# Two small layout changes and another issuer for ten small transfers in a two-block transformer kernel

## The chip, the cores and the metric

The kernel is written in Bass with its Tile layer for one Trainium2 chip, and runs on 1 core. The metric is device time in microseconds (us) of one execution; the kernel before takes 1630.53 us, the median of 3 runs. TensorE (PE) does the matrix products, VectorE (DVE) and ScalarE (ACT) the element-wise work, GpSimd (POOL) little. SyncE (SP), ScalarE and GpSimd also issue DMA transfers; "SPq", "ACTq" and "POOLq" in the rows are these issues.

## The reference

256 tokens of width 1024 pass two blocks, in float32. The first block:

```python
sh1, sc1, g1, sh2, sc2, g2 = adaln(c, w_mod, b_mod)
x = x + g1 * (concat(diff_attention, window_attention) @ w_out)
h = modulate(rmsnorm(x, norm2_g), sh2, sc2)
x = x + g2 * moe(h)          # 32 experts, the best 4 for each token
x = rmsnorm(x, final_g)
# moe, for an expert e and its tokens:
h = xb @ w_gu[e] + b_gu[e]                      # 1024 -> 2048
g = minimum(h[:, ::2], 7.0); lin = clip(h[:, 1::2], -7.0, 7.0)
y = (g * sigmoid(1.702 * g) * (lin + 1.0)) @ w_dn[e] + b_dn[e]
```

The second block is attention of three kinds (blocked, windowed, and over 256 rows of a memory `mem`), three gates, and a feed-forward part of width 2816 with a depthwise convolution:

```python
kv_me = rmsnorm(mem, norm_mem) @ w_mem_kv
s = q @ k.T * scale + bias_table[bucket(distance)]      # rel_bias
u = causal_depthwise_conv(h @ w_ffn_up, ffn_conv_w, ffn_conv_b)
y = (gelu(u_gate) * u_val) @ w_ffn_down
```

What matters here: each of the 32 experts has 8 MB of gate and up weights and 4 MB of down weights, which are all read once, 384 MB. What the second block needs of `mem`, `ffn_conv_w`, `ffn_conv_b` and `rel_bias` is small.

## The kernel before

The experts run in 16 pairs (`pair(i, bgs)`, L1419, called from the loop at L1566). A pair's two experts stand side by side in the two column halves of TensorE, with 64 slots of tokens each. For 8 values of k, 8 products (4 column groups for 2 experts, L1438) are summed in `gu`; then the activation (`swiglu_chunk`, L1163), the turning of the result, 4 steps of the down products (`dn`, L1456), and in the next pair the `combine` of the rows into the tokens (L1249).

The weights come through one ring (`Ring`, L60 to L115). A tile is 128 partitions x 8192 bytes, 1 MB; a pair needs 16 of gate and up and 8 of down, and four more tiles carry `w_mem_kv`. SyncE issues each tile's load at L99 as soon as a slot of one of the ring's pools is free (`pump`), in the order in which the products use them. The pools in the experts' part are `ra` (3 slots), `rx` (1), `rk` (1), `rb` (8, on the other side of the on-chip memory) and `rc` (3).

A transfer that SyncE or ScalarE issues signals its end on one of eight semaphores. Both engines' transfers take these in turn, in the order of the program, and a transfer waits until the one before it on the same semaphore has landed. GpSimd's transfers have eight others.

Beside the products a list of generators (`bgs`) does one step in each k step of a pair. Three of them matter here. `mem_prep` (L1263) begins in pair 1: it loads `mem` in two pieces of 128 x 1024 (`mrow`, L1268), scales its rows on VectorE (L1272 to L1276) and turns them on TensorE. `mem_kv` uses four of the ring's tiles in pairs 1 to 7. `consts_late` (L1310) is put in at pair 9 and comes to run in pairs 12 and 13: it loads the convolution's weights and bias in two halves of 88 x 128 (`V`, L1316) into a buffer that the marks `S` also use, and TensorE turns each (L494); then it loads `rel_bias` (`rb`, 32 x 16), a table `hot` (32 x 384) and `off` (16 x 384), multiplies (L1328), adds (L1329) and stores the result to `scr_bias` (L1330). All ten of these transfers are issued by ScalarE. `overflow` (L1333), after pair 0, stands under a condition that isn't met with these inputs.

Where the ring's slots lie follows from what is allotted before them: the small constants (`const`) on the one side, and `g2b` (a row of gates for all partitions, L1021) on the side of `rb`.

Of the kernel before, what the change touches and what calls it, by code (L numbers as in the profile page):

```python
# [10 lines left out]
F32 = mybir.dt.float32  # L11
F32R = mybir.dt.float32r
BF16 = mybir.dt.bfloat16
# [6 lines left out]
P = 128  # L20
D = 1024
KD = D // P
T = 256
E = 32
# [155 lines left out]
def body(tc, I, out):  # L180
# [3 lines left out]
    vec, act, pe, pool = nc.vector, nc.scalar, nc.tensor, nc.gpsimd  # L184

    def sb(stack, name, bufs=1, side=None):
        return stack.enter_context(tc.tile_pool(name=name, bufs=bufs, side=side, reuse_waits="tile"))
# [4 lines left out]
    def bc(ap1d, n, parts=P):  # L192
        return bass.AP(tensor=ap1d.tensor, offset=ap1d.offset, ap=[[0, parts], [1, n]])
# [13 lines left out]
    def rsqrt_col(dst, src, n=1, scale=1.0 / D):  # L207
        nwt[0] ^= 1
        t = newton[:, nwt[0]]
        rsqrt(dst, src, scale, (t[:, 0, :n], t[:, 1, :n]))  # L210
# [16 lines left out]
    const = sb(ex, "const")  # L227
# [220 lines left out]
    for names in ((("n1", I["norm1_g"], 8), ("bm", I["b_mod"], 40)),  # L448
                  (("n2", I["norm2_g"], 8), ("pre", I["norm_mix_pre_2"], 8), ("fpre", I["norm_ffn_pre_2"], 8),
                   ("nmem", I["norm_mem_2"], 8), ("fg", I["final_g"], 8), ("mpost", I["norm_mix_post_2"], 8), ("sub", I["subln_g"], 1))):  # L450
        V = r1.tile([sum(n for _, _, n in names), P], F32, name=f"V{len(vrows) + 1}")
# [13 lines left out]
    vec.tensor_scalar(identb, jp, 0.0, None, op0=ALU.is_equal)  # L465
    before = const.tile([P, P], BF16, name="before")
    vec.tensor_scalar(before, jp, 0.0, None, op0=ALU.is_gt)
    maskw = const.tile([P, 2, P], BF16, name="maskw")
    vec.tensor_scalar(maskw[:, 0, :], jp, 0.0, NEG, op0=ALU.is_gt, op1=ALU.mult)
    vec.tensor_scalar(maskw[:, 1, :], jp, 0.0, NEG, op0=ALU.is_lt, op1=ALU.mult)  # L470
    onesb = const.tile([P, P], BF16, name="onesb")
# [7 lines left out]
    slot = const.tile([P, SLOTS], F32, name="slot")  # L479
# [13 lines left out]
    def tp(dst, src, n=P):  # L493
        pe.transpose(dst, src, ident[:src.shape[0], :src.shape[0]])  # L494

    scrb = nc.dram_tensor("scr_bias", (16, 384), F32, kind="Internal").ap()
# [516 lines left out]
    aux = g2b = ringB_stack = None  # L1013

    def other_weights():

        nonlocal aux, g2b, ringB_stack
        rp.close()
        aux = sb(ex, "aux", side="right")
        spl.open("wo", (aux, 2), most=0)  # L1020
        g2b = aux.tile([P, D], F32, name="g2b", tag="g2b")  # L1021
        pool.dma_start(g2b, bc(I["b_mod"][0, 5120:6144], D))
        ringB_stack = ExitStack()
        ringB = sb(ringB_stack, "ringB", bufs=8, side="right")
        ring.open("rb", ringB, 8, ("qmb", 0))
        ring.pump()
        yield
# [18 lines left out]
    def warms():  # L1046
        while True:
# [3 lines left out]
    threads = {"m": mod1, "c": scale_shift(), "h": h_steps(), "1": ka_steps(0), "2": ka_steps(1), "d": small_loads(), "v": lambdas(),  # L1051
               "P": proj(), "M": mods(), "S": da_scores(), "T": da_turn(), "V": da_values(), "N": da_norm(), "W": wa_scores(),
               "s": da_probs(), "w": wa_probs(), "p": splits(), "f": flushes(), "y": warms(), "R": more_slots(), "B": other_weights(),
               "K": da_parts(), "Q": wa_parts(), "U": wa_turn(), "Z": wa_values(), "O": w_out_steps(), "X": x_turn()}

# [92 lines left out]

    vec.scalar_tensor_tensor(rk, pr[:, 0:2 * E].rearrange("p (i e) -> p i e", i=2), 1.0, sel, op0=ALU.add, op1=ALU.mult)
    vec.tensor_scalar(rk, rk, -1.0, None, op0=ALU.add)  # L1150
    cnt = const.tile([P, 4, E], F32, name="cnt")
    vec.tensor_copy(cnt[:, 0, :], pr[:, 2 * E:3 * E])
    st1.close()

# [3 lines left out]
    def misc(name="ms"):  # L1158
        return ps2.tile([P, 512], F32, name=name, tag="ms", bufs=2)
# [25 lines left out]
    xg, GT, SG, gcol = {}, {}, {}, {}  # L1185
# [30 lines left out]
    def gather(i):  # L1216

        S, G = SG.pop(i)
        xg[i] = x = l2.tile([P, KD, P], F32, name="xg", tag=f"p{i % 2}")
        for q in range(2):  # L1220
            pt = misc() if i or q else gub("ms")
            for k in range(4):
                kk = q * 4 + k
                for t in range(2):
                    pe.matmul(pt[:, k * P:(k + 1) * P], lhsT=u[:, t, kk * P:(kk + 1) * P], rhs=S[:, t, :],  # L1225
                              start=t == 0, stop=t == 1)
            for k in range(4):
                kk = q * 4 + k
                act.activation(x[:, kk, :], pt[:, k * P:(k + 1) * P], AF.Identity, scale=A2c[:, kk:kk + 1], bias=B2c[:, kk:kk + 1])  # L1229
            yield  # L1230
        pt = misc()
        if G is None:

            for t in range(2):
                tp(pt[:, t * P:(t + 1) * P], S[:, t, :])
            for t in range(2):
                pe.matmul(pt[:, T:T + 2], lhsT=S[:, t, :], rhs=ge[:, t, 2 * i:2 * i + 2], start=t == 0, stop=t == 1)
            gt = l2.tile([P, T], F32R, name="GT", tag="GT", bufs=2)
            gcol[i] = gcols[i % 2]
            for ee in range(2):  # L1240
                vec.tensor_copy(gcol[i][64 * ee:64 * ee + 64], pt[64 * ee:64 * ee + 64, T + ee:T + ee + 1])
        else:
            for t in range(2):
                tp(pt[:, t * P:(t + 1) * P], G[:, t, :])
            gt = l2.tile([P, T], F32, name="GT", tag="GT", bufs=2)
        act.activation(gt, pt[:, 0:T], AF.Copy)
        GT[i] = gt
# [14 lines left out]
    def mem_prep():  # L1262
        nonlocal memT  # L1263
        memT = aux.tile([P, KD, T], F32, name="memT", tag="ws", bufs=2)
        ms = const.tile([P, 4], F32, name="msum")
        rows_ = [l2.tile([P, D], F32, name="mrow", tag=t) for t in ("pT0", "p2")]
        for i in range(2):
            act.dma_start(rows_[i], I["mem_2"][0, i * P:(i + 1) * P, :])  # L1268
        yield
        for i, j in enumerate(rows_):  # L1270
            sq = l2.tile([P, D], F32, name="mj", tag="pT2")
            vec.tensor_tensor(sq, j, j, ALU.mult)  # L1272
            vec.tensor_reduce(ms[:, i:i + 1], sq, AX.X, ALU.add)
        rsqrt_col(ms[:, 2:4], ms[:, 0:2], 2)
        for i, j in enumerate(rows_):
            vec.tensor_scalar(j, j, ms[:, 2 + i:3 + i], None, op0=ALU.mult)  # L1276
        yield
        for i, j in enumerate(rows_):
            for q in range(2):
                pt = misc()  # L1280
                for k in range(4):
                    tp(pt[:, k * P:(k + 1) * P], j[:, (q * 4 + k) * P:(q * 4 + k + 1) * P])
                gn = colv[:, rows["nmem"]][:, q * 4:q * 4 + 4, None].to_broadcast([P, 4, P])
                vec.tensor_tensor(memT[:, q * 4:q * 4 + 4, i * P:(i + 1) * P], pt.rearrange("p (k t) -> p k t", k=4), gn, ALU.mult)
                yield
# [23 lines left out]
    def consts_late():  # L1309
        ap = I["ffn_conv_w_2"]  # L1310
        for half in range(2):
            V = l2.tile([88, P], F32, name="V2", tag="S", bufs=2)
            for q in range(2):
                n = half * 2 + q
                src = I["ffn_conv_w_2"][0, n] if n < 3 else I["ffn_conv_b_2"][0]
                act.dma_start(V[q * 44:q * 44 + 44, :], bass.AP(tensor=src.tensor, offset=src.offset, ap=[[P, 44], [1, P]]))  # L1316
            pt = misc()
            tp(pt[:, 0:88], V)
            vec.tensor_copy(conv[:, half * 2:half * 2 + 2, :], pt[:, 0:88].rearrange("p (a c) -> p a c", a=2))
            yield  # L1320
        rb = l2.tile([32, 16], F32, name="rb", tag="g", bufs=2)
        act.dma_start(rb, I["rel_bias_2"])
        hot = l2.tile([32, 384], F32, name="hot", tag="pT0")
        act.dma_start(hot, I["k_hot"])
        off = l2.tile([16, 384], F32, name="off", tag="pT2")
        act.dma_start(off, I["k_off"])
        pt = misc()
        pe.matmul(pt[0:16, 0:384], lhsT=rb, rhs=hot, start=True, stop=True)  # L1328
        vec.tensor_tensor(off, off, pt[0:16, 0:384], ALU.add)  # L1329
        act.dma_start(scrb, off)  # L1330
        yield

    def overflow():  # L1333
        nj = nc.values_load(njob[0:1, 0:1], min_val=0, max_val=15)
        with tc.If(nj > 0):
            jt = const.tile([P, 6], F32, name="jt")
            vec.memset(jt[:, 0:1], 0.0)
            eio = const.tile([P, E], F32, name="eio")
            pool.iota(eio, pattern=[[1, E]], base=0, channel_multiplier=0, allow_small_or_imprecise_dtypes=True)
            pio = const.tile([P, 1], F32, name="pio")  # L1340
            pool.iota(pio, pattern=[[0, 1]], base=0, channel_multiplier=1, allow_small_or_imprecise_dtypes=True)
            with tc.For_i(0, nj, 1):
# [219 lines left out]
    njob = const.tile([P, 1], I32, name="njob")  # L1562
    gate_values()
    SG[0] = S0, None
    gcols = [const.tile([P, 1], F32, name=f"gcol{n}") for n in range(2)]
    gather0 = gather(0)  # L1566
    next(gather0)
    bgs = []
# [413 lines left out]
    for c in range(4):  # L1982
        for m in range(2):
# [7 lines left out]
            f = 2 * c + m  # L1991
# [184 lines left out]
```

## Time and profile before

| what | value |
|---|---|
| median of 3 runs | 1630.53 us (1629.62 to 1631.3) |
| the profiled execution | 1631.8 us, span 1630.0 us |
| granted TensorE clock, mean | 0.984 of full speed |
| TensorE busy | 1565.6 us, 96% of the span |
| VectorE, ScalarE, GpSimd busy | 686.0, 487.1, 34.2 us |
| moved by DMA | 524.95 MB, mean 322 GB/s |

The page divides the span into 40 slices of 40.75 us, with a digit or a rate for each. The timeline's rows give the start, the duration, the engine, the line, the operation, the output and inputs, and behind them in brackets the idle time ahead of the instruction and what released it. A busy TensorE need not be at its peak: products that wait a little for each other, or run at a lower clock, look busy too. The share of all the span hides that the kernel has stretches of different kinds, so the windows below are cut by time.

### The profile page before, as it was taken

How to read it: one execution, taken by the hardware profiler on the slowest of the kernel's cores; microseconds unless marked ns; L12 is line 12 of the kernel's file. 1: busy time of each engine (PE TensorE's matmuls, PEld its weight loads, DVE VectorE, ACT ScalarE, POOL GpSimd, SP SyncE). 2: the span in 40 equal slices, each digit the busy share in tenths (PEclk: the TensorE clock that was granted, in tenths of full speed). 3: DMA queues.
4: the chain of work that ended last, by engine and by line, in shares of the span. 5: the costliest groups of instructions: out<-in, count | busy, mean ns of one | idle time of the engine just before them, and what ended most of it. 6: DMA issues, size and time to landing. Idle time of an engine off the chain costs nothing.

```text
span 1630.0 us, 23439 instructions
## 1 busy us (share of the span) xinstructions
PE 1565.6 (96%) x9625; PEld 948.4 (58%) x9625; DVE 686.0 (42%) x1431; ACT 487.1 (30%) x996; POOL 34.2 (2%) x39
## 2 busy tenths in 40 slices
PE   8999999899999999999999987999999999999997
PEld 6887773334433444434443432333479999899996
DVE  5877732331222212212212211122146686778786
ACT  4565532011111101101101110111045455555553
POOL 1000000000000000000000000000011001100000
PEclk9999999899999999999999997999999999999999
DMA  9758879899999999999999999899986447826651
GB/s 330 220 174 266 304 303 365 345 412 420 420 415 420 420 415 420 421 416 420 420 421 420 420 419 391 356 419 421 420 266 206 124 137 198 236 80 188 196 167 70
DMA packets 187546, 524.95 MB, mean 322 GB/s; under 512 B 11142, under 2 KB 129484, under 8 KB 138540
## 3 DMA queue, kind: packets, MB, share of 16 engines
q1 hardware_dynamic: 183600, 518.31, 83.1%
q10 hardware_dynamic: 3212, 4.14, 0.8%
q8 instruction: 77, 1.26, 0.3%
q0 software_dynamic: 624, 0.97, 0.2%
q14 instruction: 33, 0.27, 0.0%
HBM read 522.31 MB, written 1.07 MB: 321 GB/s over the span
## 4 chain that ended last, share of the span: by engine, by line
PE 68%; DMA 11%; DVE 1%; ACT 1%; issue 0%; POOL 0%; ACTq 0%; DVEq 0%; SPq 0%; POOLq 0%
PE gu L1438 23%; PE dn L1456 10%; DMA ra<-in_w_gate_up_dram 3%; PE pj L223 3%; PE pj L224 3%; PE pj L225 3%; PE ms L1225 3%; PE pv L224 3%; PE pv L223 3%; PE pv L225 3%; DMA rb<-in_w_gate_up_dram 2%; PE ms L1255 2%; PE po L224 2%; PE po L223 2%; PE po L225 2%; PE ms L494 1%
## 5 line engine op out<-in xcount | busy, mean ns | idle before, releaser
L1438 PE MATMUL gu<-rb,xg 128*64 128x512 f32 x1080 | 343.3, 612 | 0.8 <-DMA rb<-in_w_gate_up_dram 0.8
L216 DVE TENSOR_TENSOR ws<-ra,ws 128x1024 fp32r<-128x1024 f32 x146 | 176.5, 1240 | 48.2 <-ACT ws L213 48.2
L1438 PEld LDWEIGHTS gu<-rb,xg 128*64 128x64 f32 x1080 | 101.4, 140 | 146.6 <-issue 135.9
L1438 PE MATMUL gu<-ra,xg 128*64 128x512 f32 x384 | 169.1, 600 | 3.3 <-DMA ra<-in_w_gate_up_dram 2.7
L213 ACT ACTIVATE ws<-ra 128x1024 fp32r<-128x1024 f32 x146 | 148.9, 1055 | 64.9 <-PE pj L225 31.8
L1438 PE MATMUL gu<-rc,xg 128*64 128x512 f32 x424 | 164.7, 602 | 0.4 <-DMA rc<-in_w_gate_up_dram 0.4
L1229 ACT ACTIVATE xg<-ms,mcol 128x128 f32<-128x128 f32 x128 | 48.3, 458 | 381.5 <-PE ms L1225 381.5
L1456 PE MATMUL dn<-rb,aT 128*64 128x512 f32 x552 | 159.8, 597 | 0.0
L1257 DVE TENSOR_TENSOR X<-X,ms 128x512 f32<-128x512 f32 x60 | 41.2, 688 | 249.0 <-PE ms L1255 248.9
L1463 DVE SCALAR_TENSOR_TENSOR o<-dn,gcol,g2b 128x512 f32<-128x512 f32 x30 | 22.5, 751 | 212.2 <-PE dn L1456 212.2
L223 PE MATMUL pv<-fh,ws 128*128 128x256 f32 x352 | 100.2, 285 | 0.7 <-ACT fh L2023 0.7
L224 PE MATMUL pv<-fl,ws 128*128 128x256 f32 x352 | 99.6, 283 | 0.1
L225 PE MATMUL pv<-fh,ws 128*128 128x256 f32 x352 | 99.6, 283 | 0.0
L1456 PEld LDWEIGHTS dn<-rb,aT 128*64 128x64 f32 x552 | 49.3, 137 | 68.8 <-issue 66.8
L1456 PE MATMUL dn<-rc,aT 128*64 128x512 f32 x224 | 86.4, 596 | 0.0
L1438 PEld LDWEIGHTS gu<-ra,xg 128*64 128x64 f32 x384 | 46.5, 137 | 66.2 <-issue 57.9
L223 PE MATMUL pj<-hTh,ws 128*128 128x256 f32 x296 | 84.9, 287 | 0.0
L224 PE MATMUL pj<-hTl,ws 128*128 128x256 f32 x296 | 83.0, 280 | 0.0
L225 PE MATMUL pj<-hTh,ws 128*128 128x256 f32 x296 | 82.8, 280 | 0.0
L1438 PEld LDWEIGHTS gu<-rc,xg 128*64 128x64 f32 x424 | 47.4, 137 | 56.4 <-issue 51.2
L1225 PEld LDWEIGHTS ms<-S,u 128*128 128x128 f32 x512 | 59.6, 191 | 25.1 <-issue 25.1
L1438 PE MATMUL gu<-rx,xg 128*64 128x512 f32 x152 | 71.1, 597 | 0.0
(526 smaller groups left out, 2871.5 us busy)
## 6 DMA issues: line engine op xcount, KB each, us to landing
rb<-in_w_gate_up_dram SPq DMA_DIRECT2D x135, 1024.0 KB, 19.8
rb<-in_w_down_dram SPq DMA_DIRECT2D x68, 1024.0 KB, 19.8
rc<-in_w_gate_up_dram SPq DMA_DIRECT2D x53, 1024.0 KB, 19.9
ra<-in_w_gate_up_dram SPq DMA_DIRECT2D x48, 1024.0 KB, 15.1
rc<-in_w_down_dram SPq DMA_DIRECT2D x27, 1024.0 KB, 19.8
ra<-in_w_in_dram SPq DMA_DIRECT2D x26, 1024.0 KB, 5.4
ra<-in_w_ffn_up_dram SPq DMA_DIRECT2D x44, 512.0 KB, 5.3
ra<-in_w_down_dram SPq DMA_DIRECT2D x21, 1024.0 KB, 19.8
```

The source lines that it names most:

```text
L213: act.activation(hi, src, AF.Copy)
L216: vec.tensor_tensor(lo, src, hi.bitcast(F32), ALU.subtract)
L223: pe.matmul(dst, lhsT=a[0], rhs=b[0], start=start, stop=False)
L224: pe.matmul(dst, lhsT=a[0], rhs=b[1], start=False, stop=False)
L225: pe.matmul(dst, lhsT=a[1], rhs=b[0], start=False, stop=stop)
L1225: pe.matmul(pt[:, k * P:(k + 1) * P], lhsT=u[:, t, kk * P:(kk + 1) * P], rhs=S[:, t, :], start=t == 0, stop=t == 1)
L1229: act.activation(x[:, kk, :], pt[:, k * P:(k + 1) * P], AF.Identity, scale=A2c[:, kk:kk + 1], bias=B2c[:, kk:kk + 1])
L1255: pe.matmul(pt, lhsT=GT[i][:, t * P:(t + 1) * P], rhs=o[:, n * 512:(n + 1) * 512], start=j == 0, stop=j == 1)
L1257: vec.tensor_tensor(xs, xs, pt, ALU.add)
L1438: pe.matmul(gu[n][64 * ee:64 * ee + 64], lhsT=xg[i][:, k, 64 * ee:64 * ee + 64], rhs=ring.get(("gu", 2 * i + ee, k))[:, n * 512:(n + 1) * ...
L1456: pe.matmul(dn[n][64 * ee:64 * ee + 64], lhsT=aT[:, k, 64 * ee:64 * ee + 64], rhs=w[ee][:, kk, n * 512:(n + 1) * 512], start=False, stop=k ...
L1463: vec.scalar_tensor_tensor(o[:, ns], dn[n], gcol[i], g2b[:, ns], op0=ALU.mult, op1=ALU.mult)
```

## The change

There are two parts. The first moves where things lie in the on-chip memory. `cnt` takes over the place of `maskw`, which is no longer needed by then; `eio` becomes a view of `slot`, which holds the same numbers; two columns are cut out of somewhat larger tiles; and the tile of `g2b` is 120 numbers wider than what is used. By the addresses of the built programs, the constants are 576 bytes smaller per partition, so the tiles of `ra`, `rx`, `rk` and `rc`, which lay 64 bytes past a multiple of 256, now lie at a multiple of 256; those of `rb`, which lay 32 bytes past a multiple of 64 (224 past one of 256), now lie at a multiple of 512. The second part lets GpSimd issue the ten small transfers in `mem_prep` and `consts_late`.

```diff
-    maskw = const.tile([P, 2, P], BF16, name="maskw")
+    maskw = const.tile([P, 2, P], BF16, name="maskw", tag="maskw")
...
-        g2b = aux.tile([P, D], F32, name="g2b", tag="g2b")
+
+        g2b = aux.tile([P, D + 120], F32, name="g2b", tag="g2b")[:, 0:D]
...
-    cnt = const.tile([P, 4, E], F32, name="cnt")
+    cnt = const.tile([P, 4, E], F32, name="cnt", tag="maskw")
...
-            act.dma_start(rows_[i], I["mem_2"][0, i * P:(i + 1) * P, :])
+            pool.dma_start(rows_[i], I["mem_2"][0, i * P:(i + 1) * P, :])
...
-                act.dma_start(V[q * 44:q * 44 + 44, :], bass.AP(tensor=src.tensor, offset=src.offset, ap=[[P, 44], [1, P]]))
+                pool.dma_start(V[q * 44:q * 44 + 44, :], bass.AP(tensor=src.tensor, offset=src.offset, ap=[[P, 44], [1, P]]))
...
-        act.dma_start(rb, I["rel_bias_2"])
+        pool.dma_start(rb, I["rel_bias_2"])
         hot = l2.tile([32, 384], F32, name="hot", tag="pT0")
-        act.dma_start(hot, I["k_hot"])
+        pool.dma_start(hot, I["k_hot"])
         off = l2.tile([16, 384], F32, name="off", tag="pT2")
-        act.dma_start(off, I["k_off"])
+        pool.dma_start(off, I["k_off"])
...
-        act.dma_start(scrb, off)
+        pool.dma_start(scrb, off)
...
-            eio = const.tile([P, E], F32, name="eio")
-            pool.iota(eio, pattern=[[1, E]], base=0, channel_multiplier=0, allow_small_or_imprecise_dtypes=True)
+            eio = slot[:, 0:E]
...
-    gcols = [const.tile([P, 1], F32, name=f"gcol{n}") for n in range(2)]
+    gcols = [const.tile([P, n], F32, name=f"gcol{n}")[:, 0:1] for n in (24, 8)]
```

SyncE's order is the same in both programs, and so is the slot that each weight tile takes. ScalarE's rows in pairs 12 and 13 before the change, from the first load of `V` on (`xg`, `GT`: the next pair's gather; `s`, `aT`, `oh`: this pair's activation and down products):

```order
L1316 DMA V_6542<-in_ffn_conv_w_dram 44x128 x2
L1246 ACTIVATE GT<-ms 128x256
L1316 DMA V_6569<-in_ffn_conv_w_dram 44x128
L1316 DMA V_6569<-in_ffn_conv_b_dram 44x128
L1167 ACTIVATE s<-g 128x256 x4
L1473 ACTIVATE aT<-ms 128x256 x4
L1464 ACTIVATE oh<-o 128x512 x2
L1229 ACTIVATE xg<-ms,mcol 128x128 x8
L1322 DMA rb<-in_rel_bias_dram 32x16
L1324 DMA hot<-in_k_hot_dram 32x384
L1326 DMA off<-in_k_off_dram 16x384
L1330 DMA scr_bias<-off 16x384
```

And the same place of ScalarE after the change:

```order
L1247 ACTIVATE GT<-ms 128x256
L1168 ACTIVATE s<-g 128x256 x4
L1473 ACTIVATE aT<-ms 128x256 x4
L1464 ACTIVATE oh<-o 128x512 x2
L1230 ACTIVATE xg<-ms,mcol 128x128 x8
L1247 ACTIVATE GT<-ms 128x256
```

The eight transfers are gone from it, and the rest stands as it stood. GpSimd's rows after the change, from the end of `overflow` (the branch) to its first work behind the experts (`ws`, the last split of a weight tile):

```order
L1336 UNCONDITIONAL_BRANCH
L1269 DMA mrow<-in_mem_dram 128x1024 x2
L1317 DMA V_6540<-in_ffn_conv_w_dram 44x128 x2
L1317 DMA V_6567<-in_ffn_conv_w_dram 44x128
L1317 DMA V_6567<-in_ffn_conv_b_dram 44x128
L1323 DMA rb<-in_rel_bias_dram 32x16
L1325 DMA hot<-in_k_hot_dram 32x384
L1327 DMA off<-in_k_off_dram 16x384
L1331 DMA scr_bias<-off 16x384
L1552 TENSOR_TENSOR ws<-rb,ws 128x1024 x2
```

Before the change the row of `ws` follows the branch directly. Each of the ten is issued as soon as the one before it is issued and its own buffer is free.

## Rows read from the trace of the kernel before

**Rows 1.** The page's rates in 40 slices of the span.

```profile
GB/s 330 220 174 266 304 303 365 345 412 420 420 415 420 420 415 420 421 416 420 420 421 420 420 419 391 356 419 421 420 266 206 124 137 198 236 80 188 196 167 70
```

**Rows 2.** Windows: length, busy time by engine, granted clock, DMA share, GB/s.

```profile
300.00:340.00 40.00, 40.00 (x210) 16.32 (x208) 15.94 (x39) 6.11 (x16) 0.00 (x0) 0.99 0.93 371
340.00:960.00 620.00, 604.57 (x2942) 246.82 (x2939) 127.10 (x277) 81.08 (x197) 0.00 (x0) 1.00 1.01 419
960.00:1060.00 100.00, 82.97 (x384) 31.82 (x383) 16.17 (x37) 11.57 (x29) 0.00 (x0) 0.88 0.94 381
1060.00:1160.00 100.00, 98.97 (x470) 36.95 (x466) 23.14 (x48) 11.68 (x28) 0.00 (x0) 1.00 1.01 421
```

**Rows 3.** The chain that ended last: start, duration, what; two of its pieces.

```profile
351.33 3.58 PE gu L1438 x16
...
1140.29 19.84 DMA ra<-in_w_gate_up_dram
```

**Rows 4.** DMA issues: count, size of one, median us from issue to landing.

```profile
rb<-in_w_gate_up_dram SPq DMA_DIRECT2D x135, 1024.0 KB, 19.8
rb<-in_w_down_dram SPq DMA_DIRECT2D x68, 1024.0 KB, 19.8
...
mrow<-in_mem_dram ACTq DMA_DIRECT2D x2, 512.0 KB, 3.6
...
g2b<-in_b_mod_dram POOLq DMA_DIRECT2D x1, 512.0 KB, 3.9
...
bias<-in_b_gate_up_dram POOLq DMA_DIRECT2D x4, 64.0 KB, 2.1
```

**Rows 5.** Waits of SP's queue, 940 to 1070: sum, count, longest.

```profile
SPq L99 <- DMA V<-in_ffn_conv_w_dram: 17.1, 3, 11.6
...
SPq L99 <- DMA rb<-in_rel_bias_dram: 12.1, 1, 12.1
...
SPq L99 <- DMA scr_bias<-off: 4.3, 1, 4.3
```

**Rows 6.** Timeline, 972 to 997 (pair 12): start, duration, engine, line, operation.

```profile
974.15 0.55 ACTq L1316 DMA_DIRECT2D V<-in_ffn_conv_w_dram  x1
...
981.20 0.38 PE L494 MATMUL ms<-ident,V 88*128 88x88 f32 x1 [7.10 <-DMA V<-in_ffn_conv_w_dram]
981.51 6.25 PE L1438 MATMUL gu<-rb,xg 128*64 128x512 f32 x16
...
989.37 0.36 ACTq L1316 DMA_DIRECT2D V<-in_ffn_conv_b_dram  x1
...
996.01 0.38 PE L494 MATMUL ms<-ident,V 88*128 88x88 f32 x1 [7.54 <-DMA V<-in_ffn_conv_b_dram]
```

**Rows 7.** Timeline, 1036 to 1064 (pair 13).

```profile
1041.53 0.40 PE L1255 MATMUL ms<-ol,GT 128*128 128x512 f32 x1
...
1048.01 0.38 ACTq L1324 DMA_DIRECT2D hot<-in_k_hot_dram  x1
...
1049.88 0.80 PE L1328 MATMUL ms<-hot,rb 32*16 32x384 f32 x2 [2.39 <-DMA hot<-in_k_hot_dram]
```

**Rows 8.** PE's timeline: the marks' last use in pair 11, two pairs' starts.

```profile
920.72 0.51 PE L1237 MATMUL ms<-rt,S 128*128 128x2 f32 x4
...
1080.30 1.11 PE L1433 MATMUL gu<-bias,ident 32*64 32x512 f32 x16
...
1133.87 1.11 PE L1433 MATMUL gu<-bias,ident 32*64 32x512 f32 x16
```

**Rows 9.** Timeline of pair 1: the last scaling of mem's rows, their turning.

```profile
305.60 1.42 DVE L1276 TENSOR_SCALAR mrow<-mrow,msum 128x1024 f32<-128x1024 f32 x2
...
309.15 0.66 PE L494 MATMUL ms<-ident,mrow 128*128 128x128 f32 x4
```

**Rows 10.** Windows from landing to landing: three tiles of rc and rx, five of rb.

```profile
605.92:613.37 7.45, 7.45 (x42) 4.37 (x41) 0.69 (x1) 1.32 (x4) 0.00 (x0) 1.00 1.01 422
620.83:633.29 12.46, 12.46 (x62) 3.93 (x60) 5.25 (x14) 2.37 (x7) 0.00 (x0) 1.00 1.01 419
```

## The prediction

> **What bounds the kernel now.** I read the slices of the page first, then the chain, then the windows, and last the waits of SP's queue. The slices show two halves with different limits: from the ninth slice to the twenty-ninth the kernel moves 412 to 421 GB/s, with one gap of two slices (391 and 356), and then far less [rows 1]. [...] The chain's last pieces in the experts' part are weight tiles, end on end, some 19.8 us each, and the last of them ends at 1160.13 [rows 3]. A tile of 1 MB takes 19.8 us from issue to landing [rows 4], and at 420 GB/s one lands every 2.5 us, so 8 are in flight (19.8 / 2.5). The stretch 340 to 1160 is bound by SP's stream of weights; before it and after it TensorE is busy and few bytes move. There I count the change at nothing: the small loads of this diff don't reach it, but for mem's two rows, which are priced below.
>
> The gap is the one place where the stream stops with TensorE not ahead of it. Against 420 GB/s the 100 us at 381 lost (420 - 381) / 420 x 100 = **9.3 us**. The waits of SP's queue name what it stood for: the ring's next load (L99) waited on the landing of ffn_conv_w's loads for 17.1 us in three waits (the longest 11.6), of rel_bias for 12.1 us in one, of the store to scr_bias for 4.3 [rows 5]. None of these is data of a weight tile, and no free slot was missing: SP waits for these loads because in the built program ScalarE's and SP's transfers take their completion semaphores from one set of eight, in the order of the program, and each must wait for the earlier one on its semaphore. The 8 in flight are that same set. The three waits are more than the loss (33.5 against 9.3) because up to 7 tiles are still in flight while SP waits.
>
> **The change part by part.** (1) The ten small transfers. GpSimd has nothing else to do in the experts' part: in the new order its rows there are these ten and no more, and its transfers use other semaphores than SP's. So SP's waits of [rows 5] have no cause any more. SP's own order and its slots are the same as before, so the stream goes on at 420 and the 9.3 us come back: **-9.3**. ScalarE loses its issues, ten of about 0.4 us (0.55 and 0.36 in [rows 6], 0.38 in [rows 7]), which lay beside other work: 0. Bounds of this term: 0, if something else holds the stream in the gap, to -9.3; it can't be more, since all else there runs at 420.
>
> What becomes of TensorE's waits? Before, the transposes of conv_w waited 7.10 and 7.54 us, the product of hot and rel_bias 2.39 us, and after the first the 16 products took 6.25 us [rows 6, 7]; at the full clock they take 3.58 [rows 3]. The first conv_w load can now start when its buffer is free, which is after TensorE's last use of the marks S at 920.72 [rows 8], some 50 us early, so that wait goes. The second one uses the same buffer, can't be issued before the first transpose, and is wanted one k step later: 16 products of 3.58 us and the gather's last few behind them, about 4.7 together (an estimate). From ScalarE it took 996.01 - 989.37 = 6.6 us; at that, 2 us and a bit stay, say 3 with the issue. The load of hot waits for its buffer, which the last product of combine leaves at 1041.93; TensorE wants it at 1047.49 (1049.88 - 2.39) [rows 7], 5.6 us later, and ScalarE issued it only at 1048.01. At 1.9 to 6.9 us from issue to landing 0 to 1.3 stay. None of this enters the sum, and the cover is this: from 1080.30 to 1133.87 TensorE did a pair in 53.6 us [rows 8], while 24 tiles of 1.0486 MB at 420 GB/s need 59.9. TensorE thus catches up 6.3 us in a pair, 12.6 in pairs 13 and 14, and the ring has 16 slots, twice what is in flight, so the stream goes on while TensorE waits. If the cover were gone, the 3 to 4.3 us would count in full.
>
> (2) mem's two rows, which pair 1 loads. ScalarE issued them and they landed in 3.6 us; TensorE takes the result at 309.15, 2.1 us after VectorE is done with it (305.60 + 1.42 = 307.02) [rows 9]. GpSimd's nearest loads took 3.9 us for as many bytes and 2.1 us for 64 KB [rows 4]: 0.3 us later at most, inside 2.1: 0. At 300 to 340 the stream has 371 GB/s, since TensorE holds the slots [rows 2].
>
> (3) The slots. The constants shrink by 576 bytes, and g2b's tile grows by 480. By the addresses of the two programs the tiles of ra, rx, rk and rc started 64 bytes past a multiple of 256 and now start at one; those of rb started 32 past a multiple of 64, and now at a multiple of 512. No instruction changes but where it writes. What the trace has on alignment are two windows that begin and end on landings: three tiles of rc and rx in 7.45 us (2.483 each, 422 GB/s) and five of rb in 12.46 (2.492, 419 GB/s) [rows 10]. So a better start is worth 0.36% by the time, 0.7% by the bytes. rb takes 135 + 68 [rows 4] of the experts' 384 tiles, 0.53. If rb only comes up to the others: 0.53 x 0.36% x 810 us (820 less the gap's 9.3) = 1.5 us. If one more such step came for all tiles: 0.36% x 810 = 2.9 more, 4.4 in all. I take the middle, **-3.0**. Wide bounds: 2.9 us slower (the same step the other way) to 15 faster (a rival below).
>
> [...]
>
> Sum, for the profiled execution: 1631.8 - 9.3 - 3.0 = 1619.5 us. That execution was 1.3 us above the median of the timed runs, 1630.53, and so the forecast is **1618.2 us**, 0.76% faster.
>
> **The rivals.**
> A: alignment is worth far more. If each halving of the distance to a 256 byte start gave the 0.7% of the two windows [rows 10], the two steps above 422 lead to 422 x 1.007 x 1.007 = 428 GB/s, 1.9% above 420: 15.1 us on 810, with the 9.3 that is 1606.1. For it: rb and rc do differ. Against it: the difference by time is half as large, and from rb (224 past) to rc (64 past) most of the distance to 256 is gone already. [...]
>
> B: half of the gap's loss stays, because it is TensorE's stalls and not the semaphores that hold the stream: PE's waits of 7.1 and 7.5 us [rows 6] keep slots from coming free. With half of 9.3 and no gain by the slots: 1625.9. Against it: SP's waits name the loads, not a slot, and the stream's eight are no more than half of the ring.
>
> C: no change, 1630. The ten transfers still pass the same 16 engines, and the tiles pay later what they don't wait for now, while alignment is at its lower bound. Against it: 33.5 us of SP's waits in one stretch are not a matter of bytes, since the ten are about 1.2 MB together, 3 us of the stream. [...]
>
> D: slower. GpSimd's transfers queue behind the weights in flight and land as late as one of them, L = 19.8 us instead of ScalarE's 2 to 7. Then mem's rows come 19.8 - 3.6 - 2.1 = 14.1 us late, and TensorE, which sets the pace there, loses these. V's second load comes 19.8 - 4.7 = 15.1 late and hot 19.8 - 5.6 = 14.2; less the 12.6 that pairs 13 and 14 give back, 16.7. Less the terms of the sum, 12.3: 14.1 + 16.7 - 12.3 = +18.5, 1649. It decides from about L = 13.5 us: there mem's rows cost 7.8 and the two others 13.5 - 4.7 + 13.5 - 5.6 - 12.6 = 4.1, together about the 12.3 that are gained. For it: the tiles themselves take 19.8 and no row has a GpSimd load beside eight tiles. Against it: ScalarE's loads passed beside the tiles in 1.9 to 7 us [rows 6, 7], and GpSimd's known ones took 2.1 and 3.9 [rows 4].
>
> **How the numbers follow.** My forecast has 0.62, with its own range of 1612 to 1623 (the slots' term between 0 and 9). A 0.13, B 0.08, C 0.09, D 0.08. What a measurement of this kernel can tell from no change is about 0.2%, 3.3 us. Faster are the forecast, A and B: 0.83; the same is C: 0.09; slower is D: 0.08. The range takes in most of A and B and leaves out C and D: 1604 to 1626.5.
>
> **What would show it.** (1) holds if SP's waits on V, rel_bias and scr_bias are gone and the stretch about 960 to 1060 runs at 420 GB/s or more; it is wrong if that window stays near 381 with other names in SP's waits. TensorE's wait for V should be there once, of some 3 us, not twice of 7. (2) is wrong if TensorE waits for mem's rows. (3) shows in the windows on landings: below 2.483 us a tile in all pools is right, 2.49 wrong, 2.45 or less is A. What would make the whole forecast wrong is a GpSimd load that takes more than 13 us to land beside the stream, or a stretch that runs at the old rate with the gap moved elsewhere.

## The result and the profile after

The changed kernel takes 1611.38 us (median of 4 runs, 1611.04 to 1614.0) against 1630.91 in the same comparison: a ratio of 0.9885, with a 95% interval of 0.9867 to 0.9902, so 19.5 us less by the medians and 1.15% by the ratio. The forecast was 1618.2, 12.3 us less. The direction and the two places were right; the slots' term was four times too small, the other term 2.6 us too large, and a loss in the second block was not foreseen.

The profiled execution took 1611.68 us, its span 1609.9 us, with a granted clock of 0.991. Its rates by slice, which answer to [rows 1]:

```profile
GB/s 354 220 173 269 297 314 362 346 416 427 426 425 425 427 424 426 427 424 427 426 427 426 427 426 427 425 426 427 397 259 151 116 155 195 215 81 208 184 175 61
```

The two slices of 391 and 356 are gone, and the whole stretch stands at 424 to 427 where it stood at 415 to 421. In windows, as in [rows 2] (length, busy time of PE, PEld, DVE, ACT, POOL, granted clock, DMA share, GB/s):

```profile
340.00:960.00 620.00, 605.61 (x2999) 242.40 (x2997) 128.72 (x280) 82.60 (x202) 1.16 (x3) 1.00 1.01 426
960.00:1060.00 100.00, 96.19 (x456) 39.96 (x453) 22.92 (x52) 13.57 (x34) 2.94 (x6) 0.98 1.01 426
1060.00:1160.00 100.00, 97.01 (x502) 43.31 (x501) 20.58 (x46) 10.62 (x25) 0.00 (x0) 1.00 1.01 426
```

The three tiles of `rc` and `rx` and the five of `rb` that [rows 10] timed now land every 2.433 and 2.464 us:

```profile
597.27:604.57 7.30, 5.70 (x31) 2.62 (x31) 0.69 (x1) 1.51 (x4) 0.00 (x0) 1.00 1.01 429
611.91:624.23 12.32, 12.32 (x64) 3.95 (x62) 6.06 (x16) 3.19 (x8) 0.00 (x0) 1.00 1.01 424
```

Over a longer stretch, 144 tiles that SyncE issues from 566.81 to 917.88, it is 2.44 us a tile, against 2.485 for the same tiles before. A weight tile now takes 19.6 us from issue to landing, against 19.8 in [rows 4], and GpSimd's loads take 4.3 and about 5.5 (columns: count, size, median us to landing):

```profile
rb<-in_w_gate_up_dram SPq DMA_DIRECT2D x135, 1024.0 KB, 19.6
...
mrow<-in_mem_dram POOLq DMA_DIRECT2D x2, 512.0 KB, 4.3
...
V<-in_ffn_conv_w_dram POOLq DMA_DIRECT2D x3, 22.0 KB, 5.5
hot<-in_k_hot_dram POOLq DMA_DIRECT2D x1, 48.0 KB, 5.6
```

GpSimd's timeline shows how early it comes to them, against 974.15, 989.37 and 1048.01 in [rows 6, 7]; the brackets name what it waited for:

```profile
908.15 1.07 POOL L1317 DMA_DIRECT2D V<-in_ffn_conv_w_dram  x2 [614.88 <-PE ms L1238]
959.91 0.51 POOL L1317 DMA_DIRECT2D V<-in_ffn_conv_w_dram  x1 [50.69 <-PE ms L494]
960.41 0.51 POOL L1317 DMA_DIRECT2D V<-in_ffn_conv_b_dram  x1
...
1013.88 0.50 POOL L1325 DMA_DIRECT2D hot<-in_k_hot_dram  x1 [38.10 <-PE ms L1256]
```

The first loads of V go out when the marks' buffer is free, 51 us ahead of their use (959.37). The second half can only follow the first one's turning. TensorE's waits between 940 and 1070 (sum, count, longest) are these, where there were 7.5, 7.1 and 2.4 us:

```profile
PE ms L494 <- DMA V<-in_ffn_conv_b_dram: 2.3, 1, 2.3
PE gu L1438 <- DMA ra<-in_w_gate_up_dram: 1.3, 1, 1.3
PE ms L1329 <- DMA hot<-in_k_hot_dram: 0.2, 1, 0.2
```

Where the 20.1 us of the two spans come from is read by setting the same instruction of both traces side by side. First four starts of a pair (pairs 2, 6, 9 and 12) in TensorE's timeline, before and then after:

```profile
350.22 1.11 PE L1433 MATMUL gu<-bias,ident 32*64 32x512 f32 x16
...
581.89 1.11 PE L1433 MATMUL gu<-bias,ident 32*64 32x512 f32 x16
...
766.08 1.11 PE L1433 MATMUL gu<-bias,ident 32*64 32x512 f32 x16
...
945.16 1.11 PE L1433 MATMUL gu<-bias,ident 32*64 32x512 f32 x16
```

```profile
346.50 1.11 PE L1433 MATMUL gu<-bias,ident 32*64 32x512 f32 x16
...
578.16 1.11 PE L1433 MATMUL gu<-bias,ident 32*64 32x512 f32 x16
...
755.28 1.11 PE L1433 MATMUL gu<-bias,ident 32*64 32x512 f32 x16
...
931.48 1.11 PE L1433 MATMUL gu<-bias,ident 32*64 32x512 f32 x16
```

Then the experts' last products in the chain (start, duration), before and after:

```profile
1196.82 1.73 PE dn L1554 x8
```

```profile
1172.43 1.73 PE dn L1554 x8
```

The changed kernel is 3.7 us ahead at pair 2 and still 3.7 at pair 6: from pair 2 to pair 6 both need 231.7 us. It is 10.8 ahead at pair 9 and 13.7 at pair 12, and 24.4 at the experts' end. At the end of the span it is 20.1 ahead, so the second block takes 4.3 us more than before (435.7 against 431.5). There are thus four pieces: the beginning (3.7 us gained), the tiles' rate from pair 6 on, the gap, and a loss in the second block.

### The profile page after: what moved, and what is told of

Read it like the earlier page. It is cut to its first block, busy times and chain, and to the rows that moved or that the text cites. A ratio compares the mean times of both kernels' runs of the same rounds, so it can differ in the third digit from the quotient of the medians.

```text
span 1609.9 us, 23441 instructions
## 1 busy us (share of the span) xinstructions
PE 1559.9 (97%) x9625; PEld 950.0 (59%) x9625; DVE 687.0 (43%) x1431; ACT 487.3 (30%) x996; POOL 38.4 (2%) x49
## 4 chain that ended last, share of the span: by engine, by line
PE 52%; DMA 28%; DVE 1%; ACT 1%; issue 0%; POOL 0%; SPq 0%; DVEq 0%; ACTq 0%; POOLq 0%
PE gu L1438 13%; DMA rb<-in_w_down_dram 7%; DMA rb<-in_w_gate_up_dram 7%; PE dn L1456 7%; DMA ra<-in_w_gate_up_dram 5%; DMA rc<-in_w_gate_up_dram 5%; PE pj L223 3%; PE pj L224 3%; PE pj L225 3%; PE pv L224 3%; PE pv L223 3%; PE pv L225 3%; DMA rx<-in_w_gate_up_dram 2%; PE ms L1226 2%; PE po L224 2%; PE po L223 2%
## 5 line engine op out<-in xcount | busy, mean ns | idle before, releaser
L1438 PE MATMUL gu<-rb,xg 128*64 128x512 f32 x1080 | 336.7, 604 | 0.5 <-DMA rb<-in_w_gate_up_dram 0.5
## 6 DMA issues: line engine op xcount, KB each, us to landing
rb<-in_w_gate_up_dram SPq DMA_DIRECT2D x135, 1024.0 KB, 19.6
rb<-in_w_down_dram SPq DMA_DIRECT2D x68, 1024.0 KB, 19.6
rc<-in_w_gate_up_dram SPq DMA_DIRECT2D x53, 1024.0 KB, 19.5
ra<-in_w_gate_up_dram SPq DMA_DIRECT2D x48, 1024.0 KB, 19.6
rc<-in_w_down_dram SPq DMA_DIRECT2D x27, 1024.0 KB, 19.5
ra<-in_w_down_dram SPq DMA_DIRECT2D x21, 1024.0 KB, 19.5
```

The source lines that it names most:

```text
L1438: pe.matmul(gu[n][64 * ee:64 * ee + 64], lhsT=xg[i][:, k, 64 * ee:64 * ee + 64], rhs=ring.get(("gu", 2 * i + ee, k))[:, n * 512:(n + 1) * ...
```

## The experiments

**One part of the change alone.** The two kernels are the change without its second part, and without its first. Edits:

```diff
# layout only: in all six places that issue the ten transfers
-                pool.dma_start(V[q * 44:q * 44 + 44, :], ...
+                act.dma_start(V[q * 44:q * 44 + 44, :], ...
# issuer only: the kernel before with those six places changed
-                act.dma_start(V[q * 44:q * 44 + 44, :], ...
+                pool.dma_start(V[q * 44:q * 44 + 44, :], ...
```

> The change's layout with ScalarE issuing all ten small transfers as before. Theory (two parts that add up: the layout is worth the tiles' rate, the issuer is worth the gap in pairs 12 and 13): the weight tiles land every 2.44 us as after the change (2.49 before), SP still waits on V, rel_bias and scr_bias for some 30 us between 940 and 1070, and the time lies 9 to 10 us above the changed kernel's, at about 1621. Rival (the better rate fills the ring so well that the gap has no cost): within 2 us of the changed kernel, 1612. Second rival (the rate comes from the issuer, since ScalarE's small packets slow the stream): tiles at 2.49 and about 1630.

> The layout of before, GpSimd issuing the ten small transfers. Theory: tiles land every 2.486 us as before, the gap of 960 to 1060 is gone (420 GB/s there), and the time is about 1621 (1630.5 - 9.4). Rival (alignment does nothing): 1612. The second block, which took 4.3 us longer after the change than before, tells where that is from: if the layout makes it slower, this kernel has the block of before (432.4 us from the experts' last product to the end of the span); if it follows the experts' busier TensorE, it has some of the 4.3 us.

Measured: layout only 1618.89 us, ratio 0.9926 (0.9912 to 0.994); issuer only 1625.06, ratio 0.9959 (0.9946 to 0.9973). Of 1631 us that is 12.1 and 6.7 less, 18.8 together, and the whole change's 0.9885 is 18.8 too: the parts add up. Their windows over the gap, layout only and then issuer only:

```profile
960.00:1060.00 100.00, 83.23 (x392) 29.37 (x393) 19.66 (x48) 12.73 (x32) 0.00 (x0) 0.91 0.95 394
```

```profile
960.00:1060.00 100.00, 95.48 (x452) 39.61 (x448) 21.04 (x50) 13.83 (x35) 3.02 (x6) 1.00 1.01 419
```

Over 340 to 960, in the same order:

```profile
340.00:960.00 620.00, 605.68 (x2996) 243.44 (x2994) 128.35 (x279) 82.49 (x201) 0.00 (x0) 1.00 1.01 426
```

```profile
340.00:960.00 620.00, 604.98 (x2941) 243.91 (x2942) 126.97 (x277) 81.31 (x198) 1.07 (x2) 1.00 1.01 419
```

The layout raises the rate and leaves the gap; the issuer closes the gap and leaves the rate. Both theories hold, with the layout 2 us better than the 1621 I had for it and the issuer 4 us worse.

**Which tiles pay for their start.** Two kernels put one side of the ring back to its old starts:

```diff
# rb as before, 224 bytes past a multiple of 256
-        g2b = aux.tile([P, D + 120], F32, name="g2b", tag="g2b")[:, 0:D]
+        g2b = aux.tile([P, D], F32, name="g2b", tag="g2b")
# the others as before, 64 bytes past
-    gcols = [const.tile([P, n], F32, name=f"gcol{n}")[:, 0:1] for n in (24, 8)]
+    gcols = [const.tile([P, n], F32, name=f"gcol{n}")[:, 0:1] for n in (40, 8)]
```

> The changed kernel with g2b's tile at its old width, so that rb's tiles start 224 bytes past a multiple of 256 as before, and ra, rx, rk and rc at a multiple of 256. Theory (each tile pays for its own start): rb's tiles, 0.53 of all, take 2.49 us and the others 2.44, mean 2.47, and 6 us of the layout's gain in pairs 5 to 12 are lost: about 1617. Rival (the stream runs at the slowest of what is in flight): 2.486 for all, about 1622. Rival (only ra, rx, rk and rc matter): 1611.

> The changed kernel with 64 more bytes of constants, so that ra, rx, rk and rc start 64 bytes past a multiple of 256 as before, and rb at a multiple of 512. Theory (each tile pays for its own start): 0.47 of the tiles at 2.485, the others 2.44, mean 2.46, about 1616. Rival (a start at a multiple of 64 is enough, as the small difference of rb and rc before the change suggested): 2.44 for all, 1611. Rival (slowest in flight sets it): about 1622.

Measured: 1615.83 us, ratio 0.9905 (0.989 to 0.992), and 1617.38, ratio 0.9913 (0.99 to 0.9927). The windows run from landing to landing over the same tiles as [rows 10], three of rc and rx and then five of rb; first with rb's old starts:

```profile
600.25:607.54 7.29, 7.16 (x39) 4.17 (x40) 0.69 (x1) 0.90 (x4) 0.00 (x0) 1.00 1.01 427
614.96:627.43 12.47, 12.47 (x64) 3.94 (x62) 5.74 (x16) 2.70 (x7) 0.00 (x0) 1.00 1.01 421
```

and with the old starts of the others:

```profile
601.60:609.03 7.43, 6.68 (x37) 3.74 (x38) 0.69 (x1) 1.04 (x3) 0.00 (x0) 1.00 1.01 425
616.38:628.55 12.17, 12.17 (x62) 3.93 (x60) 6.07 (x16) 2.70 (x7) 0.00 (x0) 1.00 1.01 426
```

Per tile that is 2.430 and 2.494 us in the first kernel and 2.477 and 2.434 in the second. A tile pays for its own start, whatever flies beside it; the theory's 1617 and 1616 are met within 2 us. That the kernel with fewer slow tiles is the slower one lies behind the experts: their last products end at 1180.4 and 1179.9 us in the two traces, and what follows takes 433.4 and 436.3.

**Which boundary it is.** In three kernels all pools start 128, 64 or 32 bytes past a multiple of 256, and in a fourth rb starts at 256 past a multiple of 512, by the widths of the same two tiles:

```diff
# 128 past: 32 more floats in gcols, 32 fewer in g2b (64: 16; 32: 8)
+    gcols = [const.tile([P, n], F32, name=f"gcol{n}")[:, 0:1] for n in (56, 8)]
+        g2b = aux.tile([P, D + 88], F32, name="g2b", tag="g2b")[:, 0:D]
# rb at 256 past a multiple of 512
+        g2b = aux.tile([P, D + 56], F32, name="g2b", tag="g2b")[:, 0:D]
```

> The changed kernel with every pool of the ring 128 bytes past a multiple of 256 (right and left). Theory (only a start at a multiple of 256 is free, and any other start costs about the same): 2.48 us a tile, 418 to 421 GB/s in 340 to 960, about 1621. Rival (the cost grows with the distance to the boundary below): between the 64 and the 224 bytes of before, 2.485 to 2.492, 1622. Rival (128 is boundary enough): 2.44, 426 GB/s, 1611.

> The changed kernel with every pool 64 bytes past a multiple of 256. Theory (any start but a multiple of 256 costs the same): 2.48 a tile, 420 GB/s, about 1621. [...]

> The changed kernel with every pool 32 bytes past a multiple of 256, and so not at one of 64. Theory (two boundaries: 256 costs most, 64 a little more): 2.492 a tile, 419 GB/s, about 1623, as rb before the change. [...]

> The changed kernel with rb at 256 past a multiple of 512, as the other pools are, and not at a multiple of 512. Theory (256 is the boundary): 2.44 a tile, 426 GB/s, the changed kernel's time within 2 us, 1611. Rival (512 matters for rb): rb's tiles slower than 2.45, 1614 or more. It also shows whether the second block's 4 us more depend on where the right side starts: the changed kernel's 436.6 us or something else.

Measured: 1626.67 us, 1629.05, 1627.86 and 1612.69, ratios 0.9973 (0.9961 to 0.9984), 0.9988 (0.9978 to 0.9998), 0.9979 (0.9969 to 0.9988) and 0.9887 (0.9871 to 0.9904). The windows over 340 to 960, in this order:

```profile
340.00:960.00 620.00, 605.01 (x2944) 246.92 (x2940) 127.10 (x277) 80.93 (x197) 1.06 (x2) 1.00 1.01 420
```

```profile
340.00:960.00 620.00, 604.42 (x2940) 246.49 (x2936) 127.52 (x278) 80.93 (x197) 1.07 (x2) 1.00 1.01 420
```

```profile
340.00:960.00 620.00, 604.80 (x2937) 243.81 (x2935) 127.09 (x277) 81.06 (x197) 1.07 (x2) 1.00 1.01 418
```

```profile
340.00:960.00 620.00, 605.48 (x2999) 242.09 (x2997) 128.72 (x280) 83.42 (x204) 2.08 (x4) 1.00 1.01 426
```

The rate has one large step, at a multiple of 256: 426 there, 420 at 64 and at 128 past, 418 at 32 past. A multiple of 512 gives nothing more. The cost does not grow with the distance to the boundary. The first three times are 5 to 8 us above those that I expected, though the rates are as expected: the second block of these kernels is 3.8 to 6.4 us longer than before the change (436.8, 437.9 and 435.3 us, against 431.5; below), and the issuer is worth 7 us and not 9.

**What stopped the stream in the gap.** Two kernels separate the shared semaphores from TensorE's waits. In the first GpSimd issues, but a small write by ScalarE to the same buffers holds the loads of V and hot back to the place where ScalarE issued them; `rel_bias` stays early. In the second ScalarE issues V's loads, all four at once and into two buffers that are free then, and TensorE turns them ten k steps later; a third is the same with GpSimd.

```diff
# held back
             V = l2.tile([88, P], F32, name="V2", tag="S", bufs=2)
+            act.activation(V[:, 0:1], colv[0:88, 0:1], AF.Copy)
...
+        act.activation(hot[:, 0:1], colv[0:32, 0:1], AF.Copy)
# early (act in the second kernel, pool in the third)
-        for half in range(2):
-            V = l2.tile([88, P], F32, name="V2", tag="S", bufs=2)
...
+        Vs = [l2.tile([88, P], F32, name="V2", tag="G", bufs=2) for _ in range(2)]
+        for n in range(4):
...
+            act.dma_start(Vs[n // 2][n % 2 * 44:n % 2 * 44 + 44, :], ...
+        yield
+        yield
+        for half, V in enumerate(Vs):
```

> The changed kernel, GpSimd issuing, but V's and hot's buffers get a small write by ScalarE first, at the place where ScalarE issued the loads before the change, so that GpSimd can't start them earlier than that. TensorE's waits for V and hot come back (some 7, 7 and 2 to 6 us), only the semaphores are not SP's. Theory (the shared semaphores stopped the stream): SP has no waits on V, rel_bias or scr_bias, the stream runs on through TensorE's waits on the ring's free slots, and the time is 1611 to 1614. Rival (TensorE's stalls stopped the stream by holding its slots): SP waits on TensorE's products instead, 960 to 1060 stays near 395 GB/s, and the time is 1617 to 1620.

> The changed kernel with V's four loads issued by ScalarE again, but together, some ten k steps before TensorE turns them, into the two buffers that the marks G use later; rel_bias, hot, off and scr_bias stay with GpSimd. Theory (SP waits only because such a load is issued late against SP's place in the program): no wait of SP on V over 1 us, and the changed kernel's time, 1611 within 2. Rival (any load from ScalarE's queue stops SP, whenever it is issued): SP waits on V for 5 us or more, 1614 to 1617.

> As the run with ScalarE's early loads, but GpSimd issues them, so that TensorE waits for neither half of V. Theory (TensorE's 2.3 us wait after the change lies beside the stream): the wait is gone and the time the same, 1611 within 1.5. Rival (TensorE's wait counts): 1609 or less.

Measured: held back 1620.52 us, ratio 0.993 (0.9916 to 0.9943); ScalarE early 1612.17, ratio 0.9879 (0.9863 to 0.9894); GpSimd early 1613.87, ratio 0.9887 (0.9872 to 0.9902). The held-back kernel's waits of SP's queue (920 to 1070) and TensorE's in the same stretch:

```profile
SPq L99 <- PE gu L1440: 51.1, 9, 14.1
SPq L99 <- PE dn L1458: 22.8, 8, 4.2
```

```profile
PE ms L494 <- DMA V<-in_ffn_conv_w_dram: 7.9, 1, 7.9
PE ms L1331 <- DMA hot<-in_k_hot_dram: 7.0, 1, 7.0
PE ms L494 <- DMA V<-in_ffn_conv_b_dram: 6.9, 1, 6.9
```

and its window:

```profile
960.00:1060.00 100.00, 78.24 (x363) 28.12 (x363) 19.67 (x48) 12.19 (x33) 4.11 (x8) 0.86 0.99 409
```

SP waits for none of the small loads any more, and the time is that of the layout alone with ScalarE (1618.89) or a little more. TensorE's stalls are enough to cost what the gap cost. But they do not stop the stream as the gap did. It runs at full rate through both of TensorE's waits for V:

```profile
955.00:990.00 35.00, 20.28 (x80) 7.96 (x80) 2.83 (x9) 3.98 (x12) 2.09 (x4) 0.71 1.01 426
```

Only behind them do the slots run out, and SP stands for TensorE's products, 14.1 us at the longest. The stream's loss is smaller (409 GB/s against 394), and it is TensorE that ends late: it starts pair 12 2.4 us behind the changed kernel (933.91 against 931.48), and in this execution, the slowest of the five, its last products are 11.8 us behind.

In the kernel before, it was the semaphores that stopped the stream. The trace's records name the semaphore that a transfer signals: the load of `rel_bias` that goes out at 1047.60 and the tile that SP issues behind it at 1049.13 have the same one, number 102. SP's and ScalarE's 556 transfers have eight numbers between them, GpSimd's 16 have eight others. More than half of the gap's loss lies in ten microseconds, (420 - 186) / 420 x 10 = 5.6 of the 9.3 us, and in them TensorE works for 7.6. SP's row and ScalarE's issue of `rel_bias` stand beside it:

```profile
1040.00:1050.00 10.00, 7.61 (x49) 4.53 (x48) 0.69 (x1) 3.02 (x8) 0.00 (x0) 1.00 0.46 186
```

```profile
1036.67 14.59 SPq L99 DMA_DIRECT2D rb<-in_w_down_dram  x5
```

```profile
1047.60 0.32 ACTq L1322 DMA_DIRECT2D rb<-in_rel_bias_dram  x1
```

Of SP's five tiles the first goes out at 1036.67 and the second at 1049.13, after the wait of 12.1 us for `rel_bias` in [rows 5]; the other three follow within 2 us. Between 1030 and 1060 SP waits for no product of TensorE for more than 0.3 us, so slots were free. TensorE was late as well: the chain that ended last passes through its waits for both halves of V and for hot, and at 1062.85 through a slot that it frees. The gap before thus had two limits of about the same cost, a stream that stood on the semaphores and a TensorE that stood on its loads, and issuing early takes away both. TensorE's wait for hot is 7.0 us in the held-back kernel and 2.4 before, so the two can't be compared to the microsecond, and no run here has the semaphores' waits without TensorE's.

ScalarE's early loads share the semaphores with SP, and SP does wait on them, against the theory's limit of 1 us:

```profile
SPq L99 <- DMA V<-in_ffn_conv_w_dram: 6.5, 3, 4.4
SPq L99 <- DMA V<-in_ffn_conv_b_dram: 1.1, 1, 1.1
```

The time is the changed kernel's. Three waits of 2.2 us on average are about what SP waits for a weight tile (in the same kernel and stretch 17 waits of 2.1 us on average for `rb`'s gate and up tiles), as if the load only stood in a tile's place in the turn. ScalarE issues these loads at 959.88 to 961.22, 28 us into pair 12, where the first of them stood before (974.15, 29 us into it). What has changed is that the second half no longer hangs on the turning of the first, and that no product waits for either: TensorE turns them at 1019.17 and 1023.56. So it is the time between a load and its use that counts for V, and not the issuer; `rel_bias`, with the longest single wait before, was not tried in this way. The third kernel has no wait of TensorE for V at all and by the ratio is no faster (0.9887 against 0.9885): the 2.3 us that are left lie beside the stream, as forecast.

**The second block.** The last kernel pads 32 and 64 bytes behind the experts, so that the second block's two large pools start at the same place modulo 512 as before:

```diff
+    r2p = sb(rt2, "r2p", side="right")
+    pad2 = r2p.tile([P, 8], F32, name="pad2")
+    vec.memset(pad2, 0.0)
     r2 = sb(rt2, "r2", side="right")
...
+    l3p = sb(st3, "l3p")
+    pad3 = l3p.tile([P, 16], F32, name="pad3")
+    vec.memset(pad3, 0.0)
     l3 = sb(st3, "l3")
```

> The changed kernel with 64 and 32 bytes of padding that are allotted behind the experts, so that the second block's two large pools start at the same place modulo 512 bytes as before the change, while the ring's tiles of the experts keep the new starts. Theory (where those pools start makes the second block's products 1% slower): the block takes the 432 us of before instead of 436.6, and the time is 1607. Rival (it comes from elsewhere: the weights' tiles of that block or the operands kept from the experts, which still stand at their new places, or TensorE's state): 436, and 1611.

Measured: 1609.51 us, ratio 0.9865 (0.985 to 0.988). The experts' last products of the issuer-only kernel, of the one with all pools 64 past, and of this one:

```profile
1191.00 1.73 PE dn L1554 x8
```

```profile
1186.69 1.73 PE dn L1554 x8
```

```profile
1173.57 1.73 PE dn L1554 x8
```

With the spans of 1624.5, 1626.3 and 1608.1 us the rest of the kernel takes 431.8, 437.9 and 432.8 us, against 431.5 before and 435.7 after. The padding gives back 2.9 of the 4.3 us, and this is the fastest kernel measured, though by the timed runs alone its interval overlaps the changed kernel's. Each of these lengths is from one execution; the five kernels with exactly the changed layout (this change, layout only, held back, and both early ones) spread from 434.4 to 436.0, so the padding's share is 1.6 to 3.2 us. The loss is spread thin over the products of that block (columns: count, busy us, mean ns, idle); the line of before and that of after:

```profile
L224 PE MATMUL pv<-fl,ws 128*128 128x256 f32 x352 | 99.6, 283 | 0.1
```

```profile
L224 PE MATMUL pv<-fl,ws 128*128 128x256 f32 x352 | 100.4, 285 | 0.1
```

Whether the 32 or 64 bytes in where operands lie cost a product these 2 ns, and how, was not found out. The two kernels with all of the old layout have the short block (431.5 and 431.8 us); the others' is 1.3 to 6.4 us longer than before, the padded one's the least. The granted clock accounts for little of it: over the block it reads 0.99 before and 0.98 after, but also 0.98 in the padded kernel and 0.99 in layout only.

## Why the prediction was right or wrong

What bounds the kernel: right from pair 6 on, wrong for pairs 2 to 5. I took 340 to 1160 for one stretch that the stream bounds, because its rate was full. In pairs 2 to 5 TensorE sets the pace: 231.7 us in both traces with tiles that land 1.7% faster. The row of the chain that I used only for a duration, 351.33 in [rows 3], is TensorE on the chain at just that place.

The gap's term, -9.3 (its 381 GB/s is the window 960 to 1060 of [rows 2]): right in sign, too large, and its reason only half of it. Issuer only gives 6.7 us by the times, and in its trace the loads of weights gain 7.2 us between pair 11 and the experts' end (the issue of the same tile, 1.4 us behind the kernel before ahead of the gap and 5.8 us in front after it). The stretch without the gap doesn't quite run at the 420 that I set for it: 86 tiles take 216.4 us there, 2.52 each. That makes 1.7 of the 2.6 us that are missing (86 x (2.52 - 2.50), an estimate).

What stopped the stream was as I had it: no free slot was missing, and SP stood on the semaphores that it shares with ScalarE, the longest time (12.1 us) mostly while TensorE worked. What I had wrong is that these waits were the whole cause. The held-back loads cost as much without the shared set, through TensorE alone (0.993 against 0.9926 for layout only), and ScalarE's early loads of V run in the set at no cost (0.9879 against 0.9885): the lateness of the loads is the cause, and it acts in both ways. Rival B named TensorE's stalls, and left half of the loss in place; but the change takes the stalls away too, by issuing early. That most of the 9.3 us came back is therefore in part luck: I had counted on GpSimd's other semaphores for it, and these alone would not have done it.

Rival C, by which the other issuer gives nothing, holds only for the loads of V that are issued well ahead of their use: 0.9879 from ScalarE, 0.9887 from GpSimd. Where the loads stood it does not: issuer only gives 6.7 us, because GpSimd comes to the loads earlier (in the changed kernel to V's first at 908.15, ScalarE before at 974.15).

TensorE's waits: right. The first for V is gone, the second is 2.3 us (about 3 forecast), hot's 0.2 (0 to 1.3). That the rest is covered was shown by the kernel without it. The cover has its limit, though: in the held-back kernel the slots let the stream go on at 426 GB/s through two stalls of 7.9 and 6.9 us, but TensorE, which stood for 21.8 us in all, at a granted clock of 0.86 in the gap, did not catch up by the experts' end.

mem's rows: right. They land in 4.3 us, and TensorE takes them at the same distance from the pair's start as before (14.4 us before, 14.5 after). Rival D fell with this: GpSimd's loads land beside the stream in 4.3 to 5.8 us.

The slots' term, -3.0: this is the term that was mis-sized. That a better start lets the tiles land faster was right; layout only gives 12.1 us. By my own sign, 2.45 us a tile or less, the 2.44 of the long stretch is rival A and not the forecast (of the two windows on landings, 2.433 is and 2.464 is not). The time leaves the forecast's own range of 1612 to 1623 by 0.6 us, and lies in the wide one because that takes in rival A. I took the 0.36% between rb's tiles and the others' for the worth of a better start, and a second step of the same size as the most that could come. But both stood off a multiple of 256, and the step at that boundary is 1.7%, from 419 to 426 GB/s, or 0.041 us for a tile of 1.0486 MB. About 276 tiles are issued from 470 us on, where TensorE no longer holds the stream's slots, to the experts' end: 11.3 us, an estimate. The beginning gains up to 3 more, and the second block takes 3 to 4 back. How much of the beginning is the layout's is loose: kernels with all pools aligned are 1.8 to 4.9 us ahead there, those with none between 1.7 ahead and 1.0 behind. Rival A had the rate almost right (428 GB/s against 426) from a wrong rule, a gain for every halving of the distance; its time was too low because it counted the pairs that TensorE bounds and a full 9.3 for the gap, and no loss behind the experts.

Of the starts off a multiple of 256 the nearest was not the cheapest: by the windows over 340 to 960 the starts 32, 64 and 128 past cost 1.9, 1.4 and 1.4% of the rate (418, 420 and 420 GB/s against 426). The two windows of [rows 10], 224 and 64 past, thus both lay beyond the step, and their difference did not show it.

The second block's 4 us more were in none of my cases: I had counted everything behind the experts at nothing because no instruction changes there. Its operands lie elsewhere; that this is the reason rests on the padded kernel and on the two with the old layout, one execution each.

## What to carry to other kernels

Where a stream of transfers bounds a stretch, look at where its tiles start in the on-chip memory: a multiple of 256 bytes per partition was worth 1.7% of the rate here (426 GB/s against 419), and the other offsets tried lay within 0.5% of each other (418 to 420). Bound an alignment's worth by a transfer that is aligned, or call it open; the two misaligned ones here differed by 0.36%, and the step was 1.7%. Small loads beside such a stream belong to an engine that reaches them early: here late ones stalled the products that needed them by 6.9 to 7.9 us each in the held-back kernel, and before the change one of them stopped the stream that shared its semaphores for up to 12.1 us. The stalls alone cost some 7 us here (0.993 against 0.9885), and with them in place other semaphores gave nothing (0.993 against 0.9926); ask of every limit that you remove which other one stands right behind it.

## What was not expected of the hardware

The rate has one large step: 426 GB/s with starts at 256 or 512, 420 at 64 or 128 past, 418 at 32. And the second block, whose products and their order are the same in all kernels here, took from 431.5 to 437.9 us, it seems by where its operands lie; the granted clock over the block, 0.98 or 0.99, does not follow these lengths.
